# Buffers on 64-byte lines, and a head pair's first scores behind the writing of its q and k, in a hybrid decoder layer

## The chip, the cores and the metric

The kernel runs on one core of one Trainium2 chip. The metric is the device time of one execution in microseconds (us), lower is better. Below, PE is TensorE (matrix products), DVE is VectorE, ACT is ScalarE, POOL is GpSimd, and SP is the queue that issues DMA transfers.

## What is computed

One decoder layer on 512 tokens of width 2048, in float32. The normed input goes through one wide projection; half of its outputs feed an attention with 16 heads, the other half a recurrent mixer (RWKV-7); both are gated, concatenated, projected back and normed.

```python
h = rms_norm(x, norm_g[l])
proj = jnp.matmul(h, w_in[l])                                  # (512, 2048) x (2048, 8480)
q, k, v, z_att, u_shift, z_rwkv = jnp.split(proj, splits, axis=-1)
att = dilated_mixture_attention(q, k, v, pos) * jax.nn.silu(z_att)
rwk = rwkv7_time_mix(u_shift, z_rwkv, ...)                     # 16 heads of 64, state carried over time
x = x + jnp.matmul(jnp.concatenate([att, rwk], axis=-1), w_out[l])
return rms_norm(x, final_g)
```

## The kernel before

**Products in three parts.** Every float32 operand of a large product is split into a high part that PE takes in its fast float32 format and a low part with the rest. A weight chunk of 512 KB is loaded into a tile `raw`, ACT writes its high part `whi`, DVE the low part `wlo`; the input has `hh0` to `hh15` and `hl0` to `hl15`. One projected tile (`mm_k1`, `mm_qk21`, `mm_z9`: 128 outputs by 512 tokens) is 16 rounds of three matmuls, hh times whi, hl times whi, hh times wlo, from two chunks (k tiles 0 to 7 and 8 to 15).

**Stages, in this order on PE:** the recurrent mixer's projections k, r, v of 8 head pairs, with the first eight gates z0 to z7 and the recurrence's own small products between them; the attention's projections (`mm_qk00` to `mm_qk33`, in between `mv` for the values); the gates z8 to z15; the output projection `mo`, `mh`, `mt`.

**The order of instructions** is not written out by hand. All instructions are issued by one program, and each engine runs its own in that order. The big matmuls are its main line. The smaller jobs (recurrence, rope, scores, gates) are generators that are advanced between two matmuls when a small model, kept at build time (`Model`, `Engine`, `Tensor`, `Queue`), says that the time given in a `yield` has come: `yield 0.1, q` means 0.1 us after the model has `q` written. The model knows fixed costs for each engine and the reads and writes of whole tiles by name. It doesn't run on the chip: on the chip, an instruction that is issued too early waits, and all that stands behind it on its engine waits with it.

**Attention of a head pair.** `rope_evac` writes four tiles m0 to m3; `assemble` copies their rows into `qa` and `ka` by 16 DMA transfers of 64 KB on SP; ACT and DVE make from them `q` (high and low parts stacked), `kd` (k's high part) and `kl` (k's low part). `att(g)` runs the pairs 2g and 2g+1 in units of 128 queries. A unit issues, for each of two heads, a score product `s<-kd,q` and `s<-kl,q`, then DVE's masked maximum into `ss`, ACT's exponential, DVE's scaling by the sum; one unit later PE transposes `ss` into `pt`, which ACT copies to `pa` and `pb`; behind a pair's last unit comes `po`, the product with the values. `s503` is pair 5, head 0, unit 3.

**Gates.** `gate(8)` reads `mm_z8` into `zz8`, ACT's tanh goes to `zt8`, DVE multiplies into `yl8`. `gate_g(2)` makes from the weights `gw2` the parts `gh2` and `gl2` for the four matmuls `pg2`.

**Buffers.** Tiles come from rings. `k2` has 20 buffers of 128 x 520 floats (m, qa, ka, kd, kl, ss, zz, zt, yl and most other tiles of 512 columns), `k4` has 9 of 128 x 1024 (`q`, `pa`, and others). A new tile takes a buffer whose last tile has been read, and its first writer waits for that reader. PSUM has four buffers for `mm`, `mv` and `po`, and four for the rest (`s`, `pt`, `pg` in turn).

Of the kernel before, what the change touches and what calls it, by code (L numbers as in the profile page):

```python
# [11 lines left out]
F32 = mybir.dt.float32  # L12
F32R = mybir.dt.float32r
I32 = mybir.dt.int32
AF = mybir.ActivationFunctionType
ALU = mybir.AluOpType
# [4 lines left out]
P = 128  # L21
# [11 lines left out]
PV = {}  # L33
# [5 lines left out]
NPV = _o  # L39
# [97 lines left out]
def hymba_kernel(ctx: ExitStack, tc: tile.TileContext, xT, x, wa, wb, wo, pv, w2a2, g2, fg,  # L137
                 cst, rope, amask, bmask, out):
    nc = tc.nc
    ctx.enter_context(tc.manual_schedule())  # L140
    model = Model()
    V = Engine(model, nc.vector, 0.07, 0.00106, 0.18)
    S = Engine(model, nc.scalar, 0.06, 0.00095, 0.25)
# [6 lines left out]
    cp = ctx.enter_context(tc.tile_pool(name="cp", bufs=1))  # L150
    wp = ctx.enter_context(tc.tile_pool(name="wp", bufs=3))
    kp = ctx.enter_context(tc.tile_pool(name="kp", bufs=1))
# [5 lines left out]
    K1N, K2N, K4N, RAWN, AHEAD = 5, 20, 9, 2, 2  # L158

    def k2(shape, name, dt=F32):  # L160
        return kp.tile(shape, dt, tag="k2", bufs=K2N, name=name)

    def k1(shape, name, dt=F32):
        return kp.tile(shape, dt, tag="k1", bufs=K1N, name=name)
# [1 line left out]
    def k4(shape, name, dt=F32):  # L166
        return kp.tile(shape, dt, tag="k4", bufs=K4N, name=name)

    def ps(name, shape=(P, 512)):
        return pp.tile(list(shape), F32, tag="ps", name=name)  # L170

    def small(shape, name, bufs=12, dt=F32):
        return sp.tile(shape, dt, tag=f"s{shape[1]}", bufs=4 if shape[1] == 4 else bufs, name=name)

    pvt = cp.tile([P, NPV], F32, name="pvt")
    nc.scalar.dma_start(pvt, pv)

    def col(n, i):
        return pvt[:, PV[n] + i:PV[n] + i + 1]
# [5 lines left out]
    gmask = [csts[:, 320:448], csts[:, 448:576]]  # L185
    bmt = cp.tile([P, 2 * P], F32, name="bmt")
    ones = k2([P, P], "ones")
    V.memset(ones, 1.0)
    bonesr = cp.tile([P, P], F32R, name="bonesr")
    hw0 = cp.tile([P, 16], F32, name="hw0")  # L190
    nka = cp.tile([P, 8], F32, name="nka")
    omu = cp.tile([P, 27], F32, name="omu")
    V.tensor_scalar(omu, pvt[:, 0:27], -1.0, 1.0, ALU.mult, ALU.add)
    warm = cp.tile([P, 1], F32, name="warm")
    S.activation(warm, ones[:, 0:1], AF.Tanh)

    hth, htl, normed = [], [], []
    rstd = cp.tile([P, T], F32, name="rstd")
    rtok = cp.tile([P, 4], F32, name="rtok")
    xt_b, xq_b, Lb = [], [], []  # L200

    def prologue():
        acc = k2([P, T], "acc")
        xs = []

        def load_x(k):
            xs.append(k2([P, T], f"xk{k}"))
            Q.dma_start(xs[k], xT[k])
# [46 lines left out]
    def later():  # L255
        bones = k2([P, P], "bones")
        Q.dma_start(bones, cst[:, 576:704])
        Q.dma_start(bmt, bmask)
        yield 1.59, bones
        V.tensor_copy(bonesr, bones)  # L260
        V.tensor_scalar(hw0, pvt[:, PV["w0"]:PV["w0"] + 16], 0.5, None, ALU.mult)
        V.tensor_scalar(nka, pvt[:, PV["k_a"]:PV["k_a"] + 8], -1.0, None, ALU.mult)
        for i in range(2):
            G.memset(xt_b[i], 0.0)
            G.tensor_copy(Lb[i][H[i], :, H[i]], ident[H[i], H[i]][:, None, :].to_broadcast([64, NCH, C]))
            yield 0.5, G
# [136 lines left out]
    def start(gen, *wait, rank=1):  # L403
        sides.append([gen, wait_for(*(wait or (0.0,))), rank])
# [161 lines left out]
    def spill_out(key, t):  # L566
        d = dp.tile([P, T], F32, name=f"sp_{key}")
        Q.dma_start(d, t)
        spill[key] = d
# [57 lines left out]
    def pre(p, r, k, v):  # L627
# [35 lines left out]
        a = k2([P, T], f"a{p}")  # L663
# [44 lines left out]
        V.tensor_scalar(rn2, rn2, 1e-24, None, ALU.max)  # L708
        V.reciprocal(rn2, rn2)
        start(subst(p, Mp, rn2), 0.06, Mp, rn2, rank=-1)  # L710
        S.activation(a, a, AF.Identity, bias=nka[:, p:p + 1], scale=col("k_a", p))
        V.scalar_tensor_tensor(k, a, 1.0, k, ALU.add, ALU.mult)
        rk = k2([P, T], f"rk{p}")
        V.scalar_tensor_tensor(rk, r, col("r_k", p), k, ALU.mult, ALU.mult)
# [210 lines left out]
    def att_mask(t):  # L925
        return (am[0][:, 0:128], am[0][:, 128:384], am[1][:, 0:384], am[2])[t]
# [99 lines left out]
    def two(pa, t):  # L1026
        o = 256 if t == 3 else 0
        return pa[:, o:o + 768].rearrange("p (j c) -> p j c", j=2)[:, :, t * P - o:t * P - o + P]

    def att(g):  # L1030
        units = [(2 * g + pr_, t) for pr_ in range(2) for t in range(4)]
        po, ssb_, pts = {}, {}, {}
        for u in range(len(units) + 2):
            if u < len(units):
                pair, t = units[u]
                while pair not in ready or (t == 0 and u == 0 and pair >= 2 and pair - 1 not in scored):
                    yield 0.5
                tl_ = pairs[pair]
                n = max(256, 128 * (t + 1))
                nv = 128 * (t + 1)  # L1040
                tsl = slice(t * P, (t + 1) * P)
                for h in range(2):
                    sc = ps(f"s{pair}{h}{t}")
                    TE.matmul(sc[:, 0:n], tl_["q"][:, h, tsl], tl_["k", h][:, 0:n], start=True, stop=False)
                    TE.matmul(sc[:, 0:n], tl_["q"][:, h, tsl], tl_["kl", h][:, 0:n], start=False, stop=True)
                    ss = k2([P, T], f"ss{pair}{h}{t}")
                    nm = small([P, 1], f"nm{pair}{h}{t}")
                    V.tensor_tensor_reduce(ss[:, 0:nv], sc[:, 0:nv], att_mask(t), -0.125, 3.0e38,
                                           ALU.add, ALU.min, accum_out=nm)
                    den = small([P, 1], f"den{pair}{h}{t}")  # L1050
                    S.activation(ss[:, 0:nv], ss[:, 0:nv], AF.Exp, bias=nm, scale=-1.0, accum_out=den)
                    ssb_[u, h] = (ss, den)
                if t == 3:
                    scored.add(pair)
            if u >= 2:
                pair, t = units[u - 2]
                if t == 3:
                    po[pair] = pm.tile([P, T], F32, tag="mm", name=f"po{pair}")
                    for j in range(4):
                        for h in range(2):  # L1060
                            hd = (2 * pair + h) * 64
                            pa, pb = pts[pair, h]
                            pj = (pa[:, 0:512], pa[:, 512:896], pb[:, 0:256], pb[:, 256:384])[j]
                            TE.matmul(po[pair][H[h], j * P:T], vt[j][:, hd:hd + 64], pj,
                                      start=(j == 0), stop=(j == 3))
                if t == 3:
                    if f"s{pair}" in spill:
                        o = yl.pop(pair)
                        V.tensor_tensor(o, o, po.pop(pair), ALU.mult)
                    else:  # L1070
                        o = k2([P, T], f"o{pair}")
                        S.copy(o, po.pop(pair))
                    spill_out(f"o{pair}", o)
                elif t == 2 and f"s{pair}" in spill:
                    fetch_y(pair, f"s{pair}")
            if 1 <= u <= len(units):
                pair, t = units[u - 1]
                for h in range(2):
                    ss, den = ssb_.pop((u - 1, h))
                    if t == 0:  # L1080
                        pts[pair, h] = (k4([P, 1024], f"pa{pair}{h}"), k2([P, T], f"pb{pair}{h}"))
                    pa, pb = pts[pair, h]
                    pt = ps(f"pt{pair}{h}{t}")
                    for j in range(t + 1):
                        TE.transpose(pt[:, j * P:(j + 1) * P], ss[:, j * P:(j + 1) * P], ident)
                    if t == 0:
                        S.copy(pa[:, 0:P], pt[:, 0:P])
                    else:
                        S.copy(two(pa, t),
                               pt[:, 0:2 * P].rearrange("p (j c) -> p j c", j=2))  # L1090
                    if t >= 2:
                        S.copy(pb[:, (t - 2) * P:(2 * t - 3) * P], pt[:, 2 * P:(t + 1) * P])
            yield 0.0, S
            if u < len(units):
                for h in range(2):
                    ss, den = ssb_[u, h]
                    nv = 128 * (units[u][1] + 1)
                    V.reciprocal(den, den)
                    V.tensor_scalar(ss[:, 0:nv], ss[:, 0:nv], den, None, ALU.mult)
            yield 0.0, V  # L1100
# [13 lines left out]
    def fetch_y(idx, key):  # L1114
        y = k2([P, T], f"yl{idx}")
        Q.dma_start(y, spill[key])
        yl[idx] = y
# [53 lines left out]
            yield 1.05  # L1171

    fgt = []
    ssq = cp.tile([P, 4, 5], F32, name="ssq")
    yt = {}

    def residual(nb):
# [247 lines left out]
```

## Time and profile before

| | |
|---|---|
| time, median of 3 runs | 1182.05 us (1180.76 to 1182.65) |
| time of the profiled execution | 1185.02 us |
| its span (first to last instruction) | 1182.6 us |
| PE busy | 1149.7 us, 97% of the span |
| PE loading weights | 941.8 us, beside the matmuls |
| DVE, ACT, POOL busy | 742.1, 560.8, 334.1 us |
| DMA | 139.62 MB, 118 GB/s |

An engine's busy time is the time in which it had an instruction running; the rest of its span it waited. Since the matmuls of PE lie one over the other, what one costs is read from the distance of two starts, not from its own duration. All later times are of the profiled execution.

### The profile page before, as it was taken

The page shows a single profiled execution, that of the slowest core. Times are in us where ns is not written, and L with a number is a line of the kernel's source. Part 1 is how long each engine was busy: PE and PEld are TensorE (multiplying, and loading weights), DVE is VectorE, ACT ScalarE, POOL GpSimd, SP SyncE. Part 2 cuts the span into 40 slices and gives each one's busy share as a digit, 9 for nine tenths or more (in the row PEclk, how much of TensorE's full clock was granted, in tenths as well). Part 3 has the DMA queues.
Part 4 walks back from the last instruction along what each step waited for, and adds up shares of the span by engine and source line. Part 5 has one row for each costly group of instructions (what it writes and reads, how often), then busy time and mean ns, then how long its engine had stood idle before and what let it go on. Part 6 is the DMA issues. An engine that isn't in the chain of part 4 may idle for free. (4 is left out here: it accounts for less than half of the span.)

```text
span 1182.6 us, 19112 instructions
## 1 busy us (share of the span) xinstructions
PE 1149.7 (97%) x6878; PEld 941.8 (80%) x6878; DVE 742.1 (63%) x1522; ACT 560.8 (47%) x1243; POOL 334.1 (28%) x586
## 2 busy tenths in 40 slices
PE   7999999999999999999999999999899999999997
PEld 5877778788778878787799978777777778888897
DVE  5767866868786778778653546465557657243252
ACT  6455444555746655555533345435354445222243
POOL 1005883635627174653640000101010000011020
PEclk9999999999999999999999999999999999999999
DMA  7333342334242424324242354433445336444343
GB/s 260 119 95 114 115 124 73 103 100 121 66 138 72 118 95 125 105 87 111 63 120 61 112 158 132 124 110 107 119 134 148 116 116 215 123 125 130 102 125 143
DMA packets 89870, 139.62 MB, mean 118 GB/s; under 512 B 37936, under 2 KB 47664, under 8 KB 89776
## 3 DMA queue, kind: packets, MB, share of 16 engines
q1 hardware_dynamic: 89344, 137.83, 39.1%
q8 instruction: 54, 0.88, 0.3%
q10 hardware_dynamic: 432, 0.58, 0.1%
q14 instruction: 40, 0.33, 0.1%
HBM read 114.44 MB, written 14.75 MB: 109 GB/s over the span
## 5 line engine op out<-in xcount | busy, mean ns | idle before, releaser
L88 POOL TENSOR_TENSOR Xtmp<-XT,Mp 128x248 f32<-128x248 f32 (+30 forms) x248 | 132.4, 534 | 168.5 <-DVE XT L88 151.1
L88 POOL TENSOR_TENSOR XT<-XT,Xtmp 128x248 f32<-128x248 f32 (+30 forms) x248 | 139.3, 562 | 21.7 <-DVE XT L88 2.1
L121 PE MATMUL mm_qk<-hh,whi 128*128 128x512 f32 x256 | 104.8, 410 | 0.8 <-ACT gtok L88 0.8
L121 PE MATMUL mm_qk<-hl,whi 128*128 128x512 f32 x256 | 104.2, 407 | 0.0
L121 PE MATMUL mm_qk<-hh,wlo 128*128 128x512 f32 x256 | 104.1, 407 | 0.0
L121 PE MATMUL mm_z<-hh,wlo 128*128 128x512 f32 x256 | 103.2, 403 | 0.0
L121 PE MATMUL mm_z<-hl,whi 128*128 128x512 f32 x256 | 103.2, 403 | 0.0
L88 DVE TENSOR_TENSOR wlo<-raw_o,whi 128x512 fp32r<-128x512 f32 x64 | 48.0, 792 | 87.3 <-ACT whi L88 87.3
L121 PE MATMUL mm_z<-hh,whi 128*128 128x512 f32 x256 | 102.7, 401 | 0.0
L88 POOL TENSOR_TENSOR y<-y,fg 128x512 f32<-128x512 f32 (+1 forms) x16 | 19.4, 1244 | 253.5 <-DMA raw_o<-in_wo_dram 156.7
L88 ACT ACTIVATE ss<-ss,nm 128x128 f32<-128x128 f32 (+3 forms) x64 | 35.6, 556 | 105.4 <-DVE nm L88 100.8
L88 ACT ACTIVATE whi<-raw_o 128x512 fp32r<-128x512 f32 x64 | 36.9, 623 | 96.3 <-PE mo L121 73.4
L88 POOL TENSOR_TENSOR m<-m,m 128x512 f32<-128x512 f32 x16 | 22.2, 1410 | 213.4 <-DVE m L88 127.7
L121 PE MATMUL mo<-whi,mh 128*128 128x512 f32 x192 | 75.8, 395 | 0.0
L121 PE MATMUL mo<-whi,ml 128*128 128x512 f32 x192 | 75.8, 395 | 0.0
L121 PE MATMUL mo<-wlo,mh 128*128 128x512 f32 x192 | 75.8, 395 | 0.0
L88 DVE TENSOR_TENSOR wlo<-raw_v,whi 128x352 fp32r<-128x352 f32 (+1 forms) x80 | 49.5, 640 | 33.8 <-ACT whi L88 33.0
L88 DVE TENSOR_TENSOR wlo<-raw_qk,whi 128x512 fp32r<-128x512 f32 x64 | 45.0, 716 | 31.8 <-ACT whi L88 31.7
L121 PE MATMUL mv<-whi,hh 128*128 128x352 f32 x192 | 62.5, 326 | 1.1 <-DVE m L88 1.1
L121 PE MATMUL mv<-whi,hl 128*128 128x352 f32 x192 | 62.4, 325 | 0.0
L121 PE MATMUL mv<-wlo,hh 128*128 128x352 f32 x192 | 62.3, 324 | 0.0
L88 ACT ACTIVATE whi<-raw_v 128x352 fp32r<-128x352 f32 (+1 forms) x80 | 41.3, 543 | 38.8 <-PE mv L121 25.8
(304 smaller groups left out, 3033.9 us busy)
## 6 DMA issues: line engine op xcount, KB each, us to landing
raw_z<-in_wa_dram SPq DMA_DIRECT2D x32, 512.0 KB
raw_qk<-in_wa_dram SPq DMA_DIRECT2D x32, 512.0 KB
raw_o<-in_wo_dram SPq DMA_DIRECT2D x32, 512.0 KB
raw_v<-in_wb_dram SPq DMA_DIRECT2D x24, 352.0 KB
raw_r<-in_wa_dram SPq DMA_DIRECT2D x16, 512.0 KB
raw_v<-in_wa_dram SPq DMA_DIRECT2D x16, 512.0 KB
raw_k<-in_wa_dram SPq DMA_DIRECT2D x15, 512.0 KB
xk<-in_xT_dram SPq DMA_DIRECT2D x16, 256.0 KB
```

What stands on the lines that cost most here:

```text
L88: return fn(o, *args, **kw)
L121: return fn(o, lhs, rhs, **kw)
```

## The change

Every `k2` buffer becomes 528 floats wide (2112 bytes in place of 2080), and the tile is the first part of it; `pvt`, `rtok`, `ssq` grow, `warm` moves into a ring. With that every large buffer begins at a multiple of 64 bytes; before, `raw`, `whi`, `wlo`, the masks and most fixed tiles began 32 bytes off one, and the `k2` buffers by turns on and off. `nka` is no tile of its own any more: its 8 columns lie in `hw0`. And `att` yields at a pair's first unit until the model has `q` and both `kl` written. The number of instructions and what they compute stay.

```diff
     def k2(shape, name, dt=F32):
-        return kp.tile(shape, dt, tag="k2", bufs=K2N, name=name)
+        t = kp.tile([P, 528], dt, tag="k2", bufs=K2N, name=name)
+        t = t[:, 0:math.prod(shape[1:])]
+        return t if len(shape) == 2 else t.rearrange("p (a b) -> p a b", b=shape[2])
...
-    pvt = cp.tile([P, NPV], F32, name="pvt")
-    nc.scalar.dma_start(pvt, pv)
+    pvt = cp.tile([P, 112], F32, name="pvt")
+    nc.scalar.dma_start(pvt[:, 0:NPV], pv)
...
-    hw0 = cp.tile([P, 16], F32, name="hw0")
-    nka = cp.tile([P, 8], F32, name="nka")
+    hw0 = cp.tile([P, 32], F32, name="hw0")
...
-    warm = cp.tile([P, 1], F32, name="warm")
+    warm = small([P, 1], "warm")
...
-    rtok = cp.tile([P, 4], F32, name="rtok")
+    rtok = cp.tile([P, 16], F32, name="rtok")[:, 0:4]
...
-        V.tensor_scalar(hw0, pvt[:, PV["w0"]:PV["w0"] + 16], 0.5, None, ALU.mult)
-        V.tensor_scalar(nka, pvt[:, PV["k_a"]:PV["k_a"] + 8], -1.0, None, ALU.mult)
+        V.tensor_scalar(hw0[:, 0:16], pvt[:, PV["w0"]:PV["w0"] + 16], 0.5, None, ALU.mult)
+        V.tensor_scalar(hw0[:, 16:24], pvt[:, PV["k_a"]:PV["k_a"] + 8], -1.0, None, ALU.mult)
...
-        S.activation(a, a, AF.Identity, bias=nka[:, p:p + 1], scale=col("k_a", p))
+        S.activation(a, a, AF.Identity, bias=hw0[:, 16 + p:17 + p], scale=col("k_a", p))
...
                 tl_ = pairs[pair]
+                if t == 0:
+                    yield 0.1, tl_["q"], tl_["kl", 0], tl_["kl", 1]
                 n = max(256, 128 * (t + 1))
...
-    ssq = cp.tile([P, 4, 5], F32, name="ssq")
+    ssq = cp.tile([P, 4, 8], F32, name="ssq")
```

The second write into `hw0` counts, for the model, as one that follows the first, so DVE stands 0.12 us later in it from there on. Jobs are issued at other matmuls than before through the whole program. On PE the first such place is in the prologue: `prb` (its product gives `rstd`) stood ahead of the last six matmuls of `mm_v0`, and now stands behind them, directly ahead of `mm_k1`.

**The first scores of pair 4, on PE.** The matmuls are those of `mm_qk31`, and `s400` to `s410` are the scores. Before:

```order
L121 MATMUL mm_qk31_8631<-hl7_164,whi118_8489 128x512
L121 MATMUL mm_qk31_8631<-hh7_163,wlo118_8490 128x512
L121 MATMUL s400_8681<-kd_200_8668,q_20_8351 128x256
L121 MATMUL s400_8681<-kl_200_8669,q_20_8351 128x256
L121 MATMUL s410_8689<-kd_201_8672,q_20_8351 128x256
L121 MATMUL s410_8689<-kl_201_8673,q_20_8351 128x256
L121 MATMUL mm_qk31_8631<-hh8_169,whi119_8577 128x512
```

And now:

```order
L121 MATMUL mm_qk31_8630<-hh12_204,whi119_8576 128x512
L121 MATMUL mm_qk31_8630<-hl12_205,whi119_8576 128x512
L121 MATMUL s400_8710<-kd_200_8667,q_20_8349 128x256
L121 MATMUL s400_8710<-kl_200_8668,q_20_8349 128x256
L121 MATMUL s410_8718<-kd_201_8671,q_20_8349 128x256
L121 MATMUL s410_8718<-kl_201_8672,q_20_8349 128x256
L121 MATMUL mm_qk31_8630<-hh12_204,wlo119_8577 128x512
```

The four score matmuls stand 14 matmuls of `mm_qk31` further back. Pair 0's moved back by 11, pair 2's forward by 8. On DVE, pair 2's `kl_100` stood behind `yl1<-yl1,po1` (a wait for a transfer) and now stands ahead of it; pair 4's DVE rows are in the order of before.

**The gate z8, on DVE, during mm_z9.** Before (the first rows and, a little further on, the first masked maxima of pair 6; in brackets are the queues that a row waits for, DMAHW being those of transfers):

```order
L88 TENSOR_TENSOR zz8_9293<-mm_z8_9074,rstd_93 128x512 [waits PE_49]
L88 SCALAR_TENSOR_TENSOR zt8_9295<-zt8_9295,zz8_9293 128x512 [waits Activation_49]
L88 SCALAR_TENSOR_TENSOR yl8_9116<-zt8_9295,yl8_9116 128x512 [waits DVE_49]
L88 TENSOR_TENSOR wlo128_9304<-raw128_z10_9150,whi128_9303 128x512 [waits DMAHW1_49,Activation_49]
L88 TENSOR_TENSOR wlo128_9304<-raw128_z10_9150,whi128_9303 128x512 [waits Activation_49]
...
L88 ISA ss600_9363,nm600_9364<-s600_9360,L1_237 128x128 [waits PE_49]
L88 ISA nm600_9364 128x1
L88 ISA ss610_9371,nm610_9372<-s610_9368,L1_237 128x128 [waits PE_49]
L88 ISA nm610_9372 128x1
```

And now:

```order
L88 ISA ss600_9281,nm600_9282<-s600_9278,L1_236 128x128 [waits DVE_49,PE_49]
L88 ISA nm600_9282 128x1
L88 ISA ss610_9289,nm610_9290<-s610_9286,L1_236 128x128 [waits DMAHW5_49,DMAHW3_49,DMAHW7_49,DMAHW1_49,PE_49]
L88 ISA nm610_9290 128x1
L88 TENSOR_TENSOR zz8_9307<-mm_z8_9031,rstd_92 128x512 [waits DMAHW5_49,DMAHW7_49,DMAHW3_49,DMAHW1_49]
L88 SCALAR_TENSOR_TENSOR zt8_9309<-zt8_9309,zz8_9307 128x512 [waits DMAHW4_49,DMAHW2_49,DMAHW6_49,DMAHW0_49,Activation_49]
L88 SCALAR_TENSOR_TENSOR yl8_9041<-zt8_9309,yl8_9041 128x512 [waits DVE_49]
L88 TENSOR_TENSOR wlo128_9318<-raw128_z10_9117,whi128_9317 128x512 [waits Activation_49]
L88 RECIPROCAL den503_9230<-den503_9230 128x1
L88 TENSOR_SCALAR ss503_9227<-ss503_9227,den503_9230 128x512 [waits DVE_49]
```

`zz8`, `zt8` and `ss610` lie in other buffers than before: in those of `m0_31`, `m2_31` and `m0_30`, out of which SP copies pair 7's `qa_310` to `ka_311`. They wait for these transfers. On SP the 16 copies stand in one piece behind the load of `raw129`, which waits for DVE's `wlo127`, 12 rows ahead of `zz8`; before, the eight of `qa` and the eight of `ka` stood apart and `zz8` waited for none.

**The copies of pair 6's first unit, on ACT, during mm_z10.** Before:

```order
L88 ACTIVATE whi129_9377<-raw129_z10_9238 128x512 [waits DMAHW2_49,PE_49]
L88 ACTIVATE gh2_9288<-gw2_9282 128x256 [waits DMAHW6_49,DMAHW5_49,DMAHW7_49,DMAHW4_49,DMAHW0_49]
L88 ACTIVATE gl2_9289<-gw2_9282 64x128
L88 ACTIVATE whi129_9377<-raw129_z10_9238 128x512
L88 ACTIVATE ss601_9423,den601_9426<-ss601_9423,nm601_9424 128x256 [waits DVE_49]
L88 ACTIVATE ss611_9431,den611_9434<-ss611_9431,nm611_9432 128x256 [waits DVE_49,Activation_49]
L88 COPY pa60_9436<-pt600_9438 128x128 [waits PE_49]
L88 COPY pa61_9441<-pt610_9443 128x128 [waits PE_49]
L88 ACTIVATE zt9_9458<-zz9_9456 128x512 [waits DVE_49,Activation_49,Pool_49]
L88 ACTIVATE whi130_9480<-raw130_z11_9318 128x512 [waits DMAHW2_49]
```

And now:

```order
L88 COPY pa60_9403<-pt600_9405 128x128 [waits PE_49]
L88 COPY pa61_9408<-pt610_9410 128x128 [waits PE_49,Activation_49]
L88 ACTIVATE whi129_9362<-raw129_z10_9213 128x512
L88 ACTIVATE kd_310_9421<-ka_310_9267 128x512 [waits DMAHW5_49,DMAHW3_49]
L88 ACTIVATE kd_311_9425<-ka_311_9272 128x512 [waits DMAHW7_49,DMAHW1_49]
L88 ACTIVATE zt9_9457<-zz9_9455 128x512 [waits DVE_49,PE_49,Activation_49]
L88 ACTIVATE whi130_9465<-raw130_z11_9336 128x512 [waits DMAHW1_49]
L88 ACTIVATE whi130_9465<-raw130_z11_9336 128x512
L88 ACTIVATE gh2_9302<-gw2_9296 128x256 [waits DMAHW6_49,DMAHW5_49,DMAHW7_49,DMAHW4_49,DMAHW3_49]
L88 ACTIVATE gl2_9303<-gw2_9296 64x128
L88 ACTIVATE whi131_9513<-raw131_z11_9419 128x512 [waits DMAHW3_49]
```

In both, `pa61` takes the buffer of pair 5's `pa50`, which `po5` is the last to read. Before, PE issued `po5` 40 rows ahead of the transpose `pt610` from which `pa61` is copied. Now it issues it 40 rows behind, with 39 matmuls of `mm_z9` and `mm_z10` between:

```order
L121 MATMUL mm_z10_9442<-hh8_168,whi129_9362 128x512
L121 MATMUL mm_z10_9442<-hl8_169,whi129_9362 128x512
L121 MATMUL po5_9497<-pa50_9100,vt0_6183 64x512
L121 MATMUL po5_9497<-pa51_9105,vt0_6183 64x512
L121 MATMUL po5_9497<-pa50_9100,vt1_6184 64x384
```

So on ACT `pa61` now has a `po5` ahead of it that comes later, and behind it stand the second half of `whi129`, `kd_310`, `zt9`, `whi130`, `gh2`, some of which stood ahead of it before.

## Rows read from the trace of the kernel before

**Rows 1.** The page's first part: busy time, share of the span, instructions.
```profile
PE 1149.7 (97%) x6878; PEld 941.8 (80%) x6878; DVE 742.1 (63%) x1522; ACT 560.8 (47%) x1243; POOL 334.1 (28%) x586
```

**Rows 2.** Waits of PE, 40 to 690 us: total, times, longest.
```profile
PE zpb L121 <- DVE xnb L88: 1.8, 2, 1.2
PE pb L121 <- DVE l_rk L88: 1.5, 2, 1.0
...
PE mm_k L121 <- DVE u_lora L88: 0.2, 1, 0.2
```

**Rows 3.** Waits of PE, 690 to 990 us.
```profile
PE s L121 <- DVE kl L88: 6.4, 3, 3.5
PE s L121 <- ACT kd L88: 1.3, 1, 1.3
...
PE pg L121 <- DVE nm L88: 0.2, 1, 0.2
```

**Rows 4.** PE in order of time, first scores of pairs 0, 2, 4.
```profile
699.95 0.28 PE L121 MATMUL s<-kd,q 128*128 128x256 f32 x1
...
703.04 0.55 PE L121 MATMUL mm_qk<-hh,wlo 128*128 128x512 f32 x1
...
770.58 0.28 PE L121 MATMUL s<-kd,q 128*128 128x256 f32 x1
773.34 0.39 PE L121 MATMUL s<-kl,q 128*128 128x256 f32 x1 [2.48 <-DVE kl L88]
...
774.16 0.39 PE L121 MATMUL mm_qk<-hh,whi 128*128 128x512 f32 x1
...
834.45 0.28 PE L121 MATMUL s<-kd,q 128*128 128x256 f32 x1
838.22 0.38 PE L121 MATMUL s<-kl,q 128*128 128x256 f32 x1 [3.49 <-DVE kl L88]
...
839.04 0.40 PE L121 MATMUL mm_qk<-hh,whi 128*128 128x512 f32 x1
```

**Rows 5.** Stretches: PE, PEld, DVE, ACT, POOL busy (instructions), granted clock, DMA share, GB/s.
```profile
183.00:186.00 3.00, 2.17 (x14) 1.64 (x13) 2.07 (x5) 1.71 (x4) 0.23 (x2) 1.00 0.02 3
186.00:189.00 3.00, 3.00 (x18) 2.44 (x18) 0.69 (x1) 2.09 (x6) 0.00 (x0) 1.00 0.00 0
...
699.70:703.13 3.43, 1.60 (x7) 0.87 (x6) 1.50 (x4) 0.69 (x2) 0.00 (x0) 1.00 0.66 204
703.13:706.55 3.42, 3.42 (x10) 2.67 (x9) 1.04 (x4) 2.19 (x6) 0.00 (x0) 0.50 0.53 141
...
774.80:778.20 3.40, 3.40 (x9) 2.68 (x9) 2.01 (x6) 1.44 (x4) 0.00 (x0) 0.50 0.79 222
839.70:843.10 3.40, 3.40 (x9) 2.66 (x8) 2.01 (x6) 1.41 (x4) 0.00 (x0) 0.50 0.81 224
```

**Rows 6.** PE in order of time, later: spacing at either clock.
```profile
705.09 0.63 PE L121 MATMUL mm_qk<-hl,whi 128*128 128x512 f32 x1
705.52 0.63 PE L121 MATMUL mm_qk<-hh,wlo 128*128 128x512 f32 x1
...
902.15 0.39 PE L121 MATMUL mm_z<-hl,whi 128*128 128x512 f32 x1
902.38 0.28 PE L121 MATMUL s<-kd,q 128*128 128x256 f32 x1
902.50 0.28 PE L121 MATMUL s<-kl,q 128*128 128x256 f32 x1
```

**Rows 7.** DVE in order of time ahead of pair 2's kl.
```profile
768.15 0.69 DVE L88 TENSOR_TENSOR yl<-yl,po 128x512 f32<-128x512 f32 x1 [6.50 <-DMA yl<-sp_s]
...
772.61 1.28 DVE L88 TENSOR_TENSOR kl<-ka,kd 128x512 fp32r<-128x512 f32 x2
```

**Rows 8.** Tile xk: durations, min/median/max in ns.
```profile
L88 ACT ACTIVATE xk<-xk x16: 614/617/619, 26.8 to 36.7; 128x512 f32<-128x512 f32 x16
L88 DVE TENSOR_TENSOR acc<-acc,xk x14: 681/692/695, 30.1 to 42.4; 128x512 f32<-128x512 f32 x14
```

**Rows 9.** DVE in order of time behind prb, in the prologue.
```profile
58.41 0.69 DVE L88 COPY rstd<-prb 128x512 f32<-128x512 f32 x1 [3.27 <-PE prb L121]
...
59.13 0.69 DVE L88 TENSOR_TENSOR u_lora<-mm_lora,rstd 128x512 f32<-128x512 f32 x1
```

**Rows 10.** SP in order of time: pair 6's eight ka copies.
```profile
889.34 4.96 SPq L133 DMA_DIRECT2D ka<-m  x8
894.40 0.53 SPq L133 DMA_DIRECT2D raw_z<-in_wa_dram  x1
```

**Rows 11.** DVE in order of time from gate z8 on.
```profile
894.26 0.68 DVE L88 TENSOR_TENSOR zz<-mm_z,rstd 128x512 f32<-128x512 f32 x1
895.64 0.69 DVE L88 SCALAR_TENSOR_TENSOR zt<-zt,zz 128x512 f32<-128x512 f32 x1 [0.70 <-ACT zt L88]
896.37 0.69 DVE L88 SCALAR_TENSOR_TENSOR yl<-zt,yl 128x512 f32<-128x512 f32 x1
896.97 1.29 DVE L88 TENSOR_TENSOR wlo<-raw_z,whi 128x512 fp32r<-128x512 f32 x2
898.18 0.68 DVE L88 TENSOR_TENSOR yl<-yl,pg 128x512 f32<-128x512 f32 x1
```

**Rows 12.** ACT's waits for ka's transfers: total, times, longest.
```profile
ACT kd L88 <- DMA ka<-m: 4.6, 4, 1.8
```

**Rows 13.** ACT in order of time at pair 6's first copies.
```profile
908.95 0.40 ACT L88 COPY pa<-pt 128x128 f32<-128x128 f32 x2
...
911.21 0.62 ACT L88 ACTIVATE whi<-raw_z 128x512 fp32r<-128x512 f32 x1
911.73 0.62 ACT L88 ACTIVATE kd<-ka 128x512 fp32r<-128x512 f32 x1
```

## What the change is predicted to do

> **What bounds the kernel now.** I read the page's busy times first: PE works 97% of the span and DVE 63%, ACT 47% [rows 1], so only what leaves PE idle or slow counts, and a faster DVE, ACT or transfer is worth something only where PE waits for it. Next come PE's waits. From 40 to 690 us they are many and short, the longest 1.2 us [rows 2]. From 690 to 990 us nearly all of it is one line, scores that wait for `kl` (and once `kd`), and apart from these the attention and its gates cost PE 0.2 us at a `pg` [rows 3]. Then PE in order of time. Four score matmuls take 0.12 us each when nothing is late, 0.47 together [rows 6]; the first scores of pairs 0, 2, 4 took 3.09, 3.58, 4.59 us up to the next big matmul [rows 4]. The loss is 2.62 + 3.11 + 4.12 = 9.85 us. Last the granted clock: behind pair 0's stall it stands at 0.50, that is 1.2 of 2.4 GHz, for 3.42 us, after a stretch in which PE was busy 1.60 of 3.43 us [rows 5]. In it matmuls start every 0.43 us [rows 6] where the usual distance is 0.23. Eight of them fit, so it costs 8 x 0.195 = 1.55 us. The rows show such a stretch behind each of the three stalls: 4.65 us.
>
> **The alignment.** I take zero. Half of the 16 `xk` tiles lie on a 64-byte line before and half 32 bytes off, since their pitch is 2080 bytes; ACT's square on them takes 614 to 619 ns and DVE's sum 681 to 695 [rows 8]: no two groups. If alignment did speed DVE or ACT, PE's 97% would hide it but for the stalls below.
>
> Transfers are the one place where a rule speaks for a gain. SP spends 0.62 us on each `ka` copy, eight in 4.96 us, whatever tile it reads [rows 10]. The Trainium skill, "DMA: Bandwidth & Descriptors", section "How a descriptor splits into AXI transactions", says that a read which doesn't start on a 256-byte boundary needs a further transaction; after the change one `k2` buffer in four starts on one. By the rule a 2048-byte row costs 8 transactions in place of 9 there, so the 10 us of a pair's 16 copies would shrink by 10 / 9 / 4 = 0.3 us, an estimate; by the row, by nothing. Either is below what this sum can resolve.
>
> **The scores' wait, gone or nearly.** Pair 4: DVE's rows are the same, the scores come 14 matmuls later, 14 x 0.234 = 3.3 us of the 4.1. Pair 0: 11 matmuls, 2.6 us of 2.6. Pair 2: `kl` now stands ahead of `yl1`, at which DVE sat 6.50 us until 768.15, 4.5 us ahead of `kl` [rows 7], so it is written before it is needed. Left over: 0.8 us at pair 4, none to 0.5 at pair 0; I take 0.8. Such a rest should not halve the clock: the stretch from 183 to 186 us, with PE idle 3.00 - 2.17 = 0.83 us, is granted 1.00, and so is the next [rows 5]. Gain: 9.85 - 0.8 + 4.65 = 13.7 us. Bounds: 10 us (one clock drop stays, 2 us of waits stay) to 14.5.
>
> **prb behind mm_v0.** `mm_k1` takes a PSUM buffer that `u_lora` has to read first, after `rstd`: `prb` at 57.35, `rstd` 58.41 to 59.10, `u_lora` 59.13 to 59.82 [rows 9], and `mm_k1` waited 0.2 us for it [rows 2]. Six matmuls that lay in between, 1.4 us, now lie ahead of `prb`: **+1.4**.
>
> **The front half reshuffled.** Jobs of the recurrence stand at other matmuls. PE's waits there are of the size of [rows 2], about 9 us in all; some will shrink, some grow. No row prices it: bounds -3 and +4, and I take **+1.0**, since a model that has DVE later issues jobs later, and the main line waits for the recurrence's state before `mm_k6` with nothing to put in between.
>
> **Stall A, DVE at zz8.** Count from T, when `wlo127` is written. SP is then free to load `raw129` (0.5 us [rows 10]) and to issue 16 copies (9.9 us); `zz8` waits for all but the last, T + 9.8, and for its landing (ACT has waited up to 1.8 us for `ka` [rows 12]): T + 11.6. Then `zz8` to `zt8` 1.38 us, to `yl8` 0.73, to `wlo128` 0.60 [rows 11], `wlo128` 0.60, the sum's reciprocal and the scaling of `ss503` 0.7: T + 15.6, and 0.2 for the semaphores. PE meanwhile: `pt512` needs the PSUM buffer of `pg1`, which `yl9` frees, behind two `kl`: T + 1.9. From there to `pt503` stand 40 big matmuls (9.36), four short scores (0.47) and the transposes (0.33): T + 12.1. **+3.7**, between 1.5 (SP's copies begin 2 us earlier than DVE's row lets them) and 5.
>
> **Stall B, ACT at pa61.** Count from the end of `pt610`. `pa61` waits until `po5` has read `pa50`: 39 matmuls (9.1) and three of `po5` (1.2), 10.4, in which ACT does nothing. Behind it in a row: `pa61` and `whi129` 0.7 [rows 13], `wlo129` 0.6, two `kl` 1.2, two scalings 0.9, the gate z9 with `zt9` on ACT between 2.7, `wlo130` 1.2, `gl2` 0.4, `yl5` and `wlo131` 1.2 [rows 11], `ss602` 0.6, which frees the buffer of `pg2` (s602, s612, pt601, pt611 lie in the other turns): 9.5 + 0.2. So `pg2` can start at 20.1. PE is there after 9.1 + 2.2 (`po5`) + 9 matmuls 2.1 + scores 0.7 + transposes 0.4 + 0.7 of waiting for `ss601` and `ss611` (which are in the same chain): 15.2. **+4.9**, between 2.5 and 6. Short waits beside A and B, at `pt512` (it comes to `yl9` too early, 0.9), `pt601` and `pt611` (0.7), `pt612` (behind `ss602` again, 1.1): **+2.7**, between 1 and 4.
>
> **The clock behind A and B.** Both leave PE idle longer than the 2.6 us of pair 0's scores, so each should bring a stretch at half clock: 2 x 1.55 = **+3.1**. If both stalls came out below 2 us, none.
>
> **Sum**, on the profiled execution: -13.7 + 1.4 + 1.0 + 3.7 + 4.9 + 2.7 + 3.1 = +3.1 us, 1185.02 to 1188.1. That execution was 3 us above the median, of the size of the spread between executions, so I put the difference on the median: **1185.2 us**.
>
> **The rivals.** *The gain stands alone*: A and B don't come, since SP or PE run further ahead than I count and `zz8` and `pa61` find their buffers free. For it: before the change DVE and ACT had slack here, PE lost 0.2 us at the gates [rows 3]. Against: a wait of 10 us on a queue or of 39 matmuls on ACT is not covered by any slack of 2 us. -13.7 + 1.4 + 1.0 + 1 = 1171.8 us. *One of the two comes*, with its clock drop: 1177 (B gone, with its short waits) to 1179 (A gone). It needs SP to reach the copies 4 us sooner, or `po5` to find its inputs ready at a place where ACT has nothing queued. *The two losses grow*: pair 4's 0.8 us and the copies behind A push on, a third clock drop, the front half at its bound of +4: 1190 us. It decides when the waits at `pg2` pass 6 us, since then `raw131`'s load, which stands behind `wlo129` on SP, comes late for `mm_z11`. *The yield does nothing* because the model, not the chip, decides when it ends: pair 4 shows by rows that it moved, and 1199 us would follow; I give that no more than 1 in 50.
>
> **How the numbers follow.** My forecast, losses about equal to gains with 2 to 6 us over: 0.52, at 1182.5 to 1188. One of the two: 0.17. Gain alone: 0.11. Losses grow: 0.18, the one of no effect in it. 0.2%, 2.4 us, is about what a measurement can tell from no change here: that is 1179.7 to 1184.4. Faster: gain alone and most of one-of-two, 0.25. Same: the rest of that and the lower third of my forecast, 0.22. Slower: 0.53. The range that leaves out 2 in 10 goes from 1176 to 1190.
>
> **What would show it.** Right: PE's line of scores waiting for `kl` shrinks from 7.7 us to about 1; no stretch at half clock from 690 to 850 us; from z8 to z15 new waits of PE, `pt` for DVE `ss` with about 4 us and `pg` for DVE `nm` or `gl` with about 5; DVE's `zz` or `ss` waits for a transfer `ka<-m`; ACT's `pa` for PE `po` by some 7 us or more; `mm_k` for `u_lora` from 0.2 to 1.6. Wrong: no wait above 2 us behind 850 us, or half clock still behind the scores, or all durations of one form shorter than before.

## The result: 1.1% slower, and the profile after

| | before | after |
|---|---|---|
| median of the runs | 1181.4 us (1180.53 to 1182.65) | 1194.8 us (1192.75 to 1195.75) |
| ratio after / before, 95% interval | | 1.0111 (1.0096 to 1.0126) |
| time of the profiled execution | 1185.02 us | 1195.75 us |
| its span | 1182.6 us | 1193.9 us |

The forecast was 1185.2 us, 1176 to 1190. The sign was right, the size was not: the time lies 4.8 us above the range. On the profiled executions the change costs 1195.75 - 1185.02 = 10.7 us, where the sum said 3.1. One execution of a later kernel, align_only, ran at a mean granted clock of 0.655 and took 1584 us; it is left out of the figures.

PE's busy time is that of [rows 1]; the loss is time in which PE waits or is slow. The page of after, its first part:

```profile
PE 1149.3 (96%) x6878; PEld 943.6 (79%) x6878; DVE 748.2 (63%) x1510; ACT 564.4 (47%) x1255; POOL 338.8 (28%) x586
```

To see where, three places of the main line are compared in the two traces: the starts of `mm_qk10`, `mm_z8` and of the second group of `mo`'s matmuls. After, PE in order of time (start, duration):

```profile
696.32 0.50 PE L121 MATMUL mm_qk<-hh,whi 128*128 128x512 f32 x1 [0.80 <-ACT gtok L88]
...
868.80 0.39 PE L121 MATMUL mm_z<-hh,whi 128*128 128x512 f32 x1
...
1049.65 0.39 PE L121 MATMUL mo<-whi,mh 128*128 128x512 f32 x1
```

The same three matmuls start at 689.83, 876.47 and 1039.17 us in the trace of before. So:

| stretch | before | after | difference | forecast |
|---|---|---|---|---|
| up to `mm_qk10` | 689.83 | 696.32 | +6.5 | +2.4 |
| `mm_qk10` to `mm_z8` | 186.64 | 172.48 | -14.2 | -13.7 |
| `mm_z8` to `mo` | 162.70 | 180.85 | +18.15 | +14.4 |

The last two stretches don't hold the same work before and after. PE issues the `po` of pair 4 ahead of `mm_z8` (at 876.47 us) before and behind it (at 868.80 us) after; first before, then after:

```profile
871.10 1.73 PE L121 MATMUL po<-pa,vt 128*64 128x512 f32 x8
...
871.68 1.72 PE L121 MATMUL po<-pa,vt 128*64 128x512 f32 x8
```

With it, four short scores and two transposes change sides, about 2.9 us in all (2.3 of them `po`). For equal work the second stretch gains 11.3 us, and the third loses 15.3.

The waits of PE in the first stretch, 40 to 690 us (in all, times, longest), to be read beside [rows 2]:

```profile
PE Y L121 <- DVE A L88: 3.2, 2, 2.9
PE gp L121 <- ACT L L88: 2.6, 2, 2.2
PE gp L121 <- DVE L L88: 2.5, 1, 2.5
PE mm_k L121 <- DVE u_lora L88: 1.6, 1, 1.6
```

and from 690 to 1010 us, beside [rows 3]:

```profile
PE pt L121 <- DVE den L88: 5.6, 4, 3.8
PE pg L121 <- DVE nm L88: 5.0, 1, 5.0
PE pt L121 <- DVE yl L88: 0.9, 2, 0.7
PE mm_qk L121 <- ACT gtok L88: 0.8, 1, 0.8
PE s L121 <- DVE kl L88: 0.2, 1, 0.2
```

The scores' wait is gone: 7.7 us in [rows 3], now 0.2. In its place stand `pt` and `pg`, which the forecast named. New too are `gp` and a long wait at `Y` (0.8 us before), products of the recurrence, which it did not name. The stretches, as in [rows 5] (PE, PEld, DVE, ACT, POOL busy, granted clock, DMA share, GB/s):

```profile
199.50:206.30 6.80, 6.50 (x21) 5.70 (x22) 1.53 (x5) 1.69 (x5) 6.02 (x11) 0.51 0.49 137
373.60:377.00 3.40, 2.71 (x13) 2.75 (x14) 3.08 (x6) 2.69 (x6) 0.00 (x0) 0.52 0.05 11
899.10:906.00 6.90, 5.05 (x19) 4.69 (x20) 6.20 (x18) 3.69 (x11) 0.00 (x0) 0.52 0.46 152
923.00:930.00 7.00, 3.69 (x9) 2.95 (x10) 5.07 (x14) 3.22 (x10) 0.00 (x0) 0.52 0.38 114
```

None is left behind the scores; four new ones lie behind `Y`, at `gp`, behind the wait at `pt503` and behind the one at `pg2`. In the trace's record of the granted clock three of the four last 6.8 us, twice as long as those of [rows 5], and the one at `gp` 3.4; the stretches above are cut a little wider.

**Stall A as it came.** DVE in order of time (in brackets its idle time and what ended it):

```profile
891.65 0.29 DVE L88 CUSTOM_DVE_ANT_0 ss<-s,L 128x128 f32<-128x128 f32 x1 [2.28 <-DMA qa<-m]
...
896.63 0.69 DVE L88 TENSOR_TENSOR zz<-mm_z,rstd 128x512 f32<-128x512 f32 x1 [4.68 <-DMA ka<-m]
...
900.32 0.49 DVE L88 TENSOR_SCALAR ss<-ss,den 128x512 f32<-128x512 f32 x1
```

SP issues pair 7's copies in that time:

```profile
885.82 4.95 SPq L133 DMA_DIRECT2D qa<-m  x8
890.87 4.97 SPq L133 DMA_DIRECT2D ka<-m  x8
```

`zz8` starts 0.8 us behind SP's last `ka` issue, `ss503` is scaled 3.7 us behind that, and PE's `pt503` comes at once. **Stall B as it came**, on ACT, where `pa61` waits until `po5` has read `pa50`, and `whi129`, `kd_310` and `zt9` stand behind it:

```profile
906.26 0.24 ACT L88 COPY pa<-pt 128x128 f32<-128x128 f32 x1
916.19 0.27 ACT L88 COPY pa<-pt 128x128 f32<-128x128 f32 x1 [9.69 <-PE po L121]
```

and both on PE:

```profile
900.95 1.94 PE L121 MATMUL pt<-csts,ss 128*128 128x128 f32 x8 [3.78 <-DVE den L88]
...
914.38 1.72 PE L121 MATMUL po<-pa,vt 128*64 128x512 f32 x8
...
926.30 0.77 PE L121 MATMUL pg<-g128h,gh 128*128 128x512 f32 x1 [4.98 <-DVE nm L88]
926.87 0.63 PE L121 MATMUL pg<-g128l,gh 128*128 128x512 f32 x1
```

The forecast had 3.7, 10.4 and 4.9 us for the three waits; they are 3.78, 9.69 and 4.98. Behind `pg2`'s wait two matmuls start 0.57 us apart, where half clock alone gives the 0.43 of [rows 6].

### The profile page after: what moved, and what is told of

It is laid out like the page before. It is cut to its first block, busy times and chain, and to the rows that moved or that the text cites. A ratio compares the mean times of both kernels' runs of the same rounds, so it can differ in the third digit from the quotient of the medians.

```text
span 1193.9 us, 19123 instructions
## 1 busy us (share of the span) xinstructions
PE 1149.3 (96%) x6878; PEld 943.6 (79%) x6878; DVE 748.2 (63%) x1510; ACT 564.4 (47%) x1255; POOL 338.8 (28%) x586
## 5 line engine op out<-in xcount | busy, mean ns | idle before, releaser
L88 POOL TENSOR_TENSOR Xtmp<-XT,Mp 128x248 f32<-128x248 f32 (+30 forms) x248 | 134.9, 544 | 156.1 <-DVE XT L88 138.8
L88 DVE TENSOR_TENSOR wlo<-raw_z,whi 128x512 fp32r<-128x512 f32 x64 | 48.9, 784 | 29.3 <-ACT whi L88 29.2
```

Of the source, the lines that this page charges most:

```text
L88: return fn(o, *args, **kw)
```

## The experiments

My theory after the result: the yield frees the scores and pays with A and B, each with its stretch at half clock, which the forecast has right in kind; the 4 to 5 us that are missing come from the merged `nka`, which through the model's order makes `Y` and `gp` late. Rivals: the longer buffers themselves slow something; or the yield also moves the front half; or the merged tile slows the chip by itself. Every kernel here computes the whole layer. The ratio is to the kernel before, run in turn on the same chip, and not exactly the quotient of the two medians; in brackets the 95% interval. Gains in us are worked out from the ratio.

### The three parts apart

**align_only**: the lines of 64 bytes alone, `nka` a tile of its own (16 floats), no yield; the order of instructions is that of before.

```diff
+        t = kp.tile([P, 528], dt, tag="k2", bufs=K2N, name=name)
...
-    nka = cp.tile([P, 8], F32, name="nka")
+    nka = cp.tile([P, 16], F32, name="nka")
```

> The 64-byte lines alone: nka stays a tile of its own, and there is no new yield, so every engine has its instructions in the order of before. Theory (the order of instructions makes the whole difference): no change, 0.998 to 1.002 of before, the same three score stalls of 2.6 to 4.1 us and half-clock stretches behind them. Rival (part of the 5 us that the front half lost beyond the forecast is the wider or shifted buffers): 1184 to 1188 us, with PE waits before 690 us that before does not have.

Measured: 1180.85 against 1182.69 us, 0.9985 (0.9976 to 0.9994). A gain of 1.8 us, at the edge of what can be told apart. The scores wait as before:

```profile
PE s L121 <- DVE kl L88: 7.2, 4, 3.8
PE s L121 <- ACT kd L88: 1.7, 2, 1.3
```

The alignment does not make the kernel slower. Of the three half-clock stretches behind the scores this trace has two.

**merge_only**: `nka`'s columns in `hw0`, nothing else.

```diff
-    hw0 = cp.tile([P, 16], F32, name="hw0")
-    nka = cp.tile([P, 8], F32, name="nka")
+    hw0 = cp.tile([P, 32], F32, name="hw0")
```

> Only the merging of nka into hw0. Theory: the changed order of the front half costs 5 to 8 us by 690 us (mm_k for u_lora 1.6, a Y wait of 2 to 3 us near 199 us, gp waits of 2 us near 370 us, a half-clock stretch behind Y); the three score stalls stay, and no wait above 1 us comes behind z8: 1186 to 1190 us. Rival (stalls A and B come from the merge too, the yield is a pure gain): 1200 us or more.

Measured: 1188.2 us, 1.0053 (1.0036 to 1.0071), slower. Its waits from 40 to 690 us are nearly those of after:

```profile
PE Y L121 <- DVE A L88: 2.9, 2, 2.6
PE gp L121 <- ACT L L88: 2.6, 2, 2.1
PE gp L121 <- DVE L L88: 2.5, 1, 2.5
PE mm_k L121 <- DVE u_lora L88: 1.6, 1, 1.6
```

The scores wait as before, and there is no A and no B. So `Y` and `gp` are the merge's. Behind `Y` the clock is halved for 6.8 us, as in after; at `gp` it stays at 1.00, though the wait is the same 2.5 us.

**yield_only**: the yield alone.

```diff
+                if t == 0:
+                    yield 0.1, tl_["q"], tl_["kl", 0], tl_["kl", 1]
```

> Only the yield at a pair's first unit. Theory: front half as before, the score stalls and their clock gone (about -13 us), stalls A (pt, 3.7 us) and B (pg, 5 us) there with half clock behind them (+16 to +18 us): 1184 to 1187 us. Rival (A and B need the reordered front half): 1168 to 1170 us.

Measured: 1187.6 us, 1.0043 (1.0028 to 1.0057), slower. From 690 us on:

```profile
PE pt L121 <- DVE den L88: 5.5, 3, 3.8
PE pg L121 <- DVE nm L88: 5.0, 1, 5.0
PE s L121 <- DVE kl L88: 0.8, 2, 0.4
```

A and B are the yield's, and with them it costs 5 us instead of bringing the 13 of the forecast. The three parts add up to 0.81%, the whole is 1.11% (0.96 to 1.26): the parts explain most of it, and the rest is little more than their intervals. A good half of the rest has a place: in merge_only, and not in after, the matmuls of `mo` are quicker by 3.5 ns each (last section), 2.0 us or 0.17%.

### The merge: its order or its place

**merge_blind**: the same merged tile, but the model is told that its columns from 16 on are a tile of their own. The chip sees one tile, and the order is that of before.

```diff
+    def key(self, a):
+        return "nka" if a.name.startswith("hw0") and a.offset >= 16 else a.name
...
-            t = max(t, self.ready.get(a.name, 0.0))
+            t = max(t, self.ready.get(self.key(a), 0.0))
```

> nka merged into hw0 as in the change, but the build-time model is told that the two halves are different tiles, so that the order is that of before. Theory (the merge costs by the order alone): 0.998 to 1.002 of before. Rival (the shared tile itself makes an engine wait on the chip): 1186 to 1190 us like the merge.

Measured: 1178.22 against 1181.18 us, 0.9973 (0.9962 to 0.9984): faster than before. So the merge costs nothing by itself. Its order costs 1.0053 / 0.9973 = 0.8%, 9.4 us (some 2.4 either way, by the two intervals), all of it from one write that the model takes to be 0.12 us later. That the kernel is even faster than before, a little below what was expected, is not order: see the last section.

### A and B, cut one by one

**cut_a**: yield_only, with `zz8` and `zt8` in the tile of the cosines, which is free by then, so that they wait for no copy of pair 7. The model keeps its books as if they were tiles of their own, so the order is that of yield_only. **cut_b**: the same for `pa61` alone, which then needs no buffer of `po5`.

```diff
+        if idx == 8:
+            z = Lb[0].rearrange("p c t -> p (c t)")[:, 0:T]
+            model.alias[z.name] = {0: "zz8", T: "zt8"}
...
+                        if (pair, h) == (6, 1):
+                            pts[pair, h] = (Lb[0].rearrange("p c t -> p (c t)"), pts[pair, h][1])
...
```

> As the yield alone, in the same order on every engine, but zz8 and zt8 lie in the cosines' tile, which nobody needs any more, in place of the buffers that pair 7's copies read. Theory (stall A is DVE's wait for those copies): PE's pt wait of 3.8 us falls under 1, the half-clock stretch behind it goes, stall B stays: 6 to 7 us less than the yield alone, 1179 to 1182 us. Rival (DVE is late there for its own work, the wait only shows where): no change, 1187 us; or the wait moves to B, which grows by some 3 us.

Measured: 1181.02 against 1181.18 us, 0.9996 (0.9987 to 1.0004); to yield_only 0.9996 / 1.0043, 5.5 us less. `pt503`'s wait is gone, `pg2`'s stays:

```profile
PE pg L126 <- DVE nm L93: 5.0, 1, 5.0
PE pt L126 <- DVE den L93: 1.8, 3, 1.0
```

> As the yield alone, in the same order, but pa61 lies in the cosines' tile in place of pa50's buffer. Theory (stall B is ACT's wait for po5): the pg wait of 5.0 us falls under 1 and its half-clock stretch goes, stall A stays: 6 to 8 us less than the yield alone, 1179 to 1182 us. Rival (pg waits because DVE has fallen behind in stall A): no change, 1187 us.

Measured: 1178.3 us, 0.9975 (0.9966 to 0.9984), 8.0 us less than yield_only. Here it is the other way round:

```profile
PE pt L126 <- DVE den L93: 4.9, 2, 3.8
PE pt L126 <- DVE yl L93: 0.9, 2, 0.7
```

In each, one stretch of 6.83 us at half clock is left out of two. So each stall is removed by its own buffer, independently of the other, and is worth its wait and more: 5.5 us for one of 3.8, 8.0 for one of 5.0, each with some 2 us either way by the intervals. The excess, 1.7 and 3.0 us, is what the forecast had put at 1.55 each for the clock; within the intervals it is no more than that.

### The gain kept

**yield_by_pair**: the yield at pairs 0, 2 and 4 alone, each with a time of its own behind the model's writing of `kl`. The order around the pairs 6 and 7 differs from both before and after: `po5` stands 21 matmuls behind `pt610`, where in yield_only it stands 40 behind, and `zz8` and `zt8` lie in buffers that pair 7's copies don't read.

```diff
+    LAT = {0: 0.8, 2: 0.1, 4: 3.0}
...
+                if t == 0 and pair in LAT:
+                    yield LAT[pair], tl_["q"], tl_["kl", 0], tl_["kl", 1]
```

> As the yield alone, but with 0.8 us for pair 0, 0.1 for pair 2, 3.0 for pair 4 and none for the others. Theory (A and B hang on where the later jobs happen to fall, not on the scores being late as such): by the order pair 7's copies and po5 no longer meet zz8 and pa61 there; score waits under 1 us, no wait above 1.5 us behind z8, 1168 to 1173 us. Rival (scores that are issued later always push the gates into A and B): 1182 us or more.

Measured: 1173.81 against 1182.69 us, 0.9931 (0.9917 to 0.9945): 8.2 us faster by the ratio. From 690 us on no wait for a score is left, nor one over 1.1 us:

```profile
PE pt L121 <- DVE den L88: 3.7, 5, 1.1
PE pt L121 <- DVE ss L88: 0.9, 1, 0.9
```

No stretch at half clock is left but the one at the end. ACT's `pa61` still waits 4.8 us for `po5`, but `pg2` now stands ahead of `po5` and PE doesn't feel it. The idea of the change was worth a gain of 8 us; where the later pairs' jobs fell took it back.

### On lines of 64 bytes, in four places

The next kernels add to yield_by_pair what moves tiles in SBUF, the order kept. **by_pair_aligned** takes the edits of align_only. **by_pair_off64** is the same with `nka` 32 floats wide, which puts `raw`, `whi`, `wlo` and the `k2` buffers 64 bytes further. **by_pair_off192** has `rtok` in `nka`'s tile instead, which puts them 64 bytes the other way. **by_pair_blind** has merge_blind's tile and the old `k2` buffers of 2080 bytes.

```diff
-    nka = cp.tile([P, 16], F32, name="nka")
+    nka = cp.tile([P, 32], F32, name="nka")
```

> The yields of 0.8, 0.1 and 3.0 us for pairs 0, 2 and 4, now with all buffers on 64-byte lines and nka apart; the order is that of the yields by pair alone. Theory (alignment gives a small gain of its own, 0.1 to 0.2%): 1171 to 1173 us, 1 to 3 us under the yields by pair. Rival (what the lines alone showed was a matter of which executions had a half-clock stretch more): 1173 to 1175 us, the same ratio 0.993.

> As the yields by pair with all buffers on 64-byte lines, but raw, whi, wlo and the k2 ring 64 bytes further on: 64 past a 256-byte line in place of 0. Theory (PE's pace depends on where the weights lie): mo's matmuls are 1 to 3% closer than 233 ns, and mm's stay at 232.5: 1169 to 1171 us. Rival (the pace of mo in the merged kernels had another reason, the k2 ring's pitch among them): 233 ns and 1172 us as with the lines alone.

> The same with raw, whi, wlo and the k2 ring at 192 past a 256-byte line, where raw, whi and wlo of the merged kernels lie; rtok lies in nka's tile. Theory (it is the place of whi and wlo): mo's three kinds of matmuls are at 229, 226 and 232 ns as in the merged kernels, mm's at 232.5 to 233.1: 1169 to 1171 us. Rival (it needs the ring's old pitch, or masks 32 bytes off): 233 ns, 1172 us.

> The yields by pair on the kernel with nka merged into hw0 and the model told that they are two tiles: k2 keeps its pitch of 2080 bytes, raw, whi, wlo lie at 192. Theory: the gains add, 8 us from the yields and 2.5 to 3 us from mo: 1170 to 1172 us. Rival (the merged tile's 3 us came from executions with fewer half-clock stretches): 1173 to 1175 us.

| kernel | `whi` begins at, modulo 256 bytes | median, us | ratio |
|---|---|---|---|
| yield_by_pair | 160 | 1173.81 | 0.9931 (0.9917 to 0.9945) |
| by_pair_aligned | 0 | 1172.1 | 0.9923 (0.9911 to 0.9935) |
| by_pair_off64 | 64 | 1166.64 | 0.9874 (0.9858 to 0.9891) |
| by_pair_off192 | 192 | 1173.27 | 0.9923 (0.9911 to 0.9936) |
| by_pair_blind | 192 | 1171.33 | 0.9909 (0.9896 to 0.9923) |

The intervals of the other four overlap. by_pair_off64 is 0.4 to 0.6% faster than they are, and the fastest kernel of this study: 1166.64 us, 15 less than before. The gain lies in the matmuls themselves (last section), but in other ones than I had expected: `mo` was to become quicker and `mm` to stay, and it is the `mm` that became quicker while `mo` stayed at 233 ns. For by_pair_off192 I had expected a quick `mo` too, and it stayed at 233 ns; there the rival, 1172 us, came closest.

## Why the prediction was right or wrong

**The scores' wait and its clock, -13.7: held, and the stretch still gained less.** By the measure of the forecast, the time up to the next big matmul less 0.47 us, the first scores lose 0.85 us at pair 4 where I kept 0.8, 0.4 at pair 0 and nothing at pair 2, and no half clock followed: that is 9.85 - 1.25 + 4.65 = 13.25 us. But for equal work the stretch gained 11.3, since the transposes of pair 0's first units wait now (1.1 us at `pt` by the trace, and some time lost around them). The forecast had such short waits only behind `mm_z8`.

**`mm_k1`, +1.4: held.** It waits 1.6 us where it waited 0.2.

**Stalls A and B, +3.7 and +4.9, short waits +2.7: held.** Place, order of causes and size of the two came out: 3.78 and 4.98. All of PE's waits at `pt` and `pg` are 5.6 + 0.9 + 5.0 = 11.5 us against a sum of 11.3, but 1.1 of them lie ahead of `mm_z8`; behind it they are 10.4, of which 1.6 are the short ones that I had at 2.7. cut_a and cut_b show that the two buffers named are the causes. The yield alone makes both; the merge has no part in them.

**"The front half reshuffled, +1.0": failed, and it is the step that took the time out of the range.** I bounded it at -3 to +4 by the total of [rows 2] and took a value near the middle. PE's waits from 40 us up to `mm_qk10` add up to 9.2 us before and 15.3 after, 6.1 more, of which 1.4 is `mm_k1`'s: +4.7, past the bound. And two of the new waits bring stretches at half clock, which I had counted behind A and B and forgotten here: 6.8 us behind `Y`, 3.4 at `gp`. At 1.55 us for each 3.4 that is 4.65 us, if PE lost there what it lost in [rows 5]. Against it stands one such stretch at 23.9 us that before had and after has not, about 1.3 us: `mm_v` begins at 45.33 in place of 46.67. The sum, 1.4 + 4.7 + 4.65 - 1.3 = 9.45, is 2.9 above the 6.5 measured; about 1.1 of that is the quicker matmuls below (some 1800 of them here, 0.6 ns each), the rest stays open. merge_only against merge_blind shows the same cost without the other edits: the order that the merge brings costs 9.4 us, where I had 1.4 + 1.0. I had said that no row prices the reshuffle; that was true, but the order of after was there to be read, and I followed it row by row only from pair 0 on. `Y` could have been counted there as A and B were.

**"The clock behind A and B, +3.1": too small.** Two stretches came, as said, but of 6.8 us each in place of 3.4. PE worked in them from 900.95 to 906.2 and from 926.30 to 930.1 us; at 0.43 us from start to start in place of 0.23 that loses about 2.5 and 1.8, 4.3 us, an estimate. With the waits of 10.4 this gives 14.7 of the 15.3 us that the third stretch lost for equal work.

**The base.** I put the difference on the median, although the profiled execution of before stood 3.0 us above it. The profiled one of after stands only 1.0 us above its own, so the medians differ by 13.4 us where the profiles differ by 10.7. A difference of two single executions carries both their scatters; I knew of one of them and left it out of the range. The clock is part of that scatter: align_only, merge_only and merge_blind have the scores late as before, and each of their traces shows two half-clock stretches behind them, not three. So the 4.65 us that I counted are those of one execution, and probably more than the kernel loses on the mean.

**"The alignment, zero": about right for the wrong reason.** I argued that DVE, ACT and transfers gain nothing that PE does not hide, and nothing of the kind can be seen: SP still takes 4.97 us for eight `ka` copies, 4.96 in [rows 10]. So the Trainium skill's rule in "DMA: Bandwidth & Descriptors", section "How a descriptor splits into AXI transactions", shows no effect in that row. But the row times SP's issuing; whether the transfers behind it became shorter, no run here was made to show. The 1.8 us of align_only lie elsewhere: PE itself is quicker, 0.6 ns for each of 2688 matmuls or 1.6 us (last section), which I had not thought of.

**The rivals.** "The losses grow" was the one that came, but only in part by its mechanism: the front half at its bound and more clock drops were in it, while `pg2`'s wait stayed below the 6 us from which I had it decide. "The gain stands alone" is what yield_by_pair comes near to, with the later pairs not held back: 8.2 us of the 13.7, since waits of 4.6 us at `pt` remain.

## What to carry to other kernels

Where a model at build time sets the order, one write that the model puts 0.12 us later can cost more than an edit saves: hold the order fixed (tell the model the old story) and time the rest, before a gain or loss is put down to the edit. When work is moved later to end a wait, follow the buffers that it holds to the next tiles that take them, on every engine that stands in a row behind those tiles, and price each new wait of PE of some 2 us or more, in every part of the kernel, with the slow clock that may come behind it. Before two stretches of a trace are compared, see that they hold the same work. Then end the wait only where it costs, pair by pair.

## What the runs showed of the hardware that was not expected

**PE's pace changes with the place of the tiles, in kernels with the same order of instructions.** Worked out from the starts in the traces, as the mean distance of two that lie less than 260 ns apart at full clock: the matmuls of the projected tiles (`mm_r` to `mm_z`, `mm_qk`, 2688 in all) take 233.1 ns in before, 232.6 in by_pair_aligned, and 228.8 to 230.5 in by_pair_off64; of `mm_z` and `mm_qk`, yield_by_pair, merge_blind and by_pair_off192 have the first value, align_only the second. Between by_pair_aligned and by_pair_off64 that is about 3.1 ns for each, 8.3 us. PE's waits from 40 to 690 us take back 2.3 of it (9.4 us in all in the one, 11.7 in the other): a quicker PE comes earlier to the recurrence. Those from 690 us on are 0.8 shorter (4.0 and 3.2), and one stretch at half clock, which by_pair_aligned has not, takes about 1.55; it is shown below. That leaves 5.2 us; the spans of the two traces differ by 5.0, the medians by 5.5. The costliest groups (busy time, mean ns of one) show it as well, in by_pair_aligned:

```profile
L121 PE MATMUL mm_z<-hl,whi 128*128 128x512 f32 x256 | 103.0, 402 | 0.0
...
L121 PE MATMUL mo<-whi,ml 128*128 128x512 f32 x192 | 75.8, 395 | 0.0
```

in by_pair_off64:

```profile
L121 PE MATMUL mm_z<-hl,whi 128*128 128x512 f32 x256 | 102.5, 400 | 0.0
```

and in merge_blind, where it is `mo` that is quicker:

```profile
L124 PE MATMUL mo<-whi,ml 128*128 128x512 f32 x192 | 74.5, 388 | 0.0
```

`mo`'s starts lie 225.9 to 231.7 ns apart in merge_blind, merge_only and by_pair_blind, and 233 in before, align_only and the other kernels with the yield by pair; 576 matmuls at 4.4 ns less are 2.5 us, most of what merge_blind gains. For `mo` it is not the place of PE's own operands that decides: by_pair_off192 and by_pair_blind issue the same 576 matmuls in the same order, and `whi`, `wlo`, `mh`, `ml` and the PSUM buffers lie at the same addresses in both, yet their mean distances are 233.3 and 228.9 ns. What differs between the two is the place of other tiles, the `k2` buffers above all. For the projected tiles, by_pair_off64 is the one kernel with the weights at 64 bytes, and the `k2` buffers moved with them; which of the two makes it quick is not shown. How either comes about stays open.

**The slow clock.** The stretches at half clock, the one at the end of each trace left out, were 3.4 or 6.8 us long, 6.8 behind three of the new stalls, of 2.9 to 5.0 us. In by_pair_off64 one came behind a wait of 1.9 us, PE's only one from 700 to 715 us:

```profile
PE pt L121 <- DVE den L88: 1.9, 1, 1.9
...
708.70:712.10 3.40, 3.40 (x10) 2.62 (x9) 2.21 (x4) 1.78 (x3) 0.00 (x0) 0.50 0.65 181
```

And an equal stall does not always bring one: the wait of 2.5 us at `gp` halved the clock in after and not in merge_only. In align_only, pair 0's scores leave PE as idle as in [rows 5], and the clock behind them stays whole:

```profile
696.00:699.40 3.40, 1.16 (x3) 0.56 (x3) 1.37 (x3) 0.83 (x2) 0.00 (x0) 1.00 0.61 179
699.40:702.80 3.40, 3.33 (x15) 2.74 (x16) 0.68 (x6) 1.81 (x6) 0.00 (x0) 1.00 0.55 161
```
